# A new order for a mixer's products: keys and receptances of both head groups first, values and pool as filling, and an output projection that starts with the recurrence's rows

## The chip, the cores and the metric

The kernel runs on one core of a Trainium2 chip. The metric is the device time in microseconds of one execution, taken from several runs; the profile is one further execution with the hardware profiler on.

## The reference

One layer of a hybrid decoder trunk on 256 tokens of width 2048, all in float32:

```
h = rms_norm(x, attn_norm);  z = h @ w_in                    # 2048 -> 4384
d = causal_multiscale_pool(z[:, :1024])                      # 4 windows
pool_out = (d @ pool_w, per window) * pool_scale
r, k, v, w, a, g = token_shift(z[:, 1024:], mu_shift)        # 16 heads of 64
decay, a, g from low-rank products of w, a, g;  kk = normalised k * k_k
per token:  S = S * decay + (S @ -kk) (kk * a)^T + v k^T;    y = S @ r
y = group_norm(y) * gn_g + gn_b + sum(r * k * r_k) * v;      rwkv_out = y * g
x = x + concat(pool_out, rwkv_out) @ w_out
x = x + relu(rms_norm(x) @ w_ffn_up)^2 @ w_ffn_down          # width 8192
x = x + sigmoid(rms_norm(x) @ w_ple_gate) * (p @ w_ple_proj)
return rms_norm(x, final_norm)
```

## The kernel before

Each weight matrix is streamed once in panels of 512 KB (two row tiles of 128 by 512 columns). A panel is loaded into a ring `raw`, and split into a high part by ScalarE (`wh`, line 168) and a remainder by VectorE (`wl`, line 169), each ring three deep in the mixer. Every product is then made of three matmuls: high by high, high by low, low by high. `gemm_cols` keeps the output columns on the partitions (lines 181 to 183: zk, zr, zv), `gemm_toks` the tokens (lines 190 to 192: the pool's zp and w_out's o). Both take two of three PSUM banks `mm`; the next product can begin on the third, and goes on when the first two have been evacuated.

The mixer is about the first quarter of the run. In it the order of TensorE is written out by hand (`manual_schedule`): its matmuls run in the order in which the program issues them. The other engines, and the queue of DMA issues (SP), are ordered by a scheduler by priorities and its own estimates; evacuations and splits have raised priority.

The 16 heads are two groups (index 0 and 1) of eight. The recurrence is computed in four chunks of 64 tokens. The steps of a group, in the order of the program:

- `rwkv_lora`: low-rank products (L529), sigmoids, a running sum, two exponentials on ScalarE.
- `rwkv_k`: squares, sums over heads (`kkn`), a root, their spread (`rnb`, L497), and VectorE's products into the tiles AR and BK. It fills 6.4 and 4.6 us between these. `rwkv_r`: the same for r, and `rk`.
- `rwkv_scores`: chunk scores `sc` (L623), masked by VectorE into SC, with 2.6 us of filling between the chunks. `rwkv_sources`: BK scaled and transposed (`bkt`, L653).
- `bonus_sums` (tile `bs`, one buffer) and `rwkv_values`: the spread of the bonus (`bon`, L497), and the transposed, centred values (`vt`, L747), copied to UV.

Then, for both groups at once: `inverse`, a triangular inverse of 32 by 32 blocks, 31 dependent pairs of VectorE operations between transposes; `rwkv_merge` (products `gm` and `qm`, lines 708 and 717, with ScalarE copies into T1G and SC); and `rwkv_core`. In each of its four steps the core makes `dy`, evacuates R, makes `us` from R, evacuates UV (half on ScalarE, half on VectorE), updates the state from `us` and adds to `dy`. Behind these stand the fills whose sizes the change alters (1.5, 1.5, 1.8). After steps 1 and 3 `group_norm` treats one half of the tokens.

The tail of the mixer: `pool_chunk` (band products `pd`, lines 920 and 924), `group_out` (transposes `yt`, line 868, with scale and bias), `pool_mix` (`pm`), `rwkv_gates` (`gt`, lines 887 and 891) from the weight tile `gu`, which has one buffer and is loaded by `gate_load`, and `rwkv_out`, which multiplies the gates in and splits the result into `mg`. w_out takes its 16 row tiles from `mix`: 0 to 7 are the pool's (`mp`), 8 to 15 the recurrence's (`mg`); a panel covers two of them (`kps`).

The filling works by generators. Each `gemm_` function yields after a unit (0.36 us for column products, 0.68 for token products). `queued` puts it on a list; `fill(us)` takes units from the head of the list until the amount is reached or the list is empty; `finish(gen)` takes units until that product is done; `run` does a product at once. While the inverse is pending (`beside`), every 1.0 us of units also issues its next step, so `while beside: fill(1.0)` goes on until all its steps are issued. Before, the list is zk0, zr0, zv0, zk1, zr1, zv1, zp0, zp1; later two pieces of the first quarter of w_out (its pool rows) are queued as well and fill the tail.

Of the kernel before, what the change touches and what calls it, by code (L numbers as in the profile page):

```python
# [16 lines left out]
T = 256  # L17
# [23 lines left out]
def trunk(  # L41
# [221 lines left out]
    def fill(us):  # L263

        while us > 0 and queue:
            us -= advance()

    def finish(gen):
        while any(g is gen for g in queue):
            advance()  # L270
# [451 lines left out]

    def bonus_sums(gi, st):
        nb = head_sums(st["rk"], "bsum", 1)
        st["bs"] = rp.tile([128, T], F32, tag="sq", name=f"bs{gi}")
        with tc.high_priority(30000):
            nc.scalar.activation(st["bs"], nb, AF.Copy)

# [23 lines left out]
    def rwkv_core(sts):  # L752

        Rs = rp.tile([128, 2, 8, 64], F32, tag="tD", name="R")
        yss = [rp.tile([128, 2, 8, 64], F32, tag=tg, name=f"ys{gi}") for gi, tg in enumerate(("tE", "zv"))]
        SCs, UVs, ARs, BKts = ([st[k] for st in sts] for k in ("SC", "UV", "AR", "BKt"))

        def half(b, rows, part):
            return b[rows, part * 256 : part * 256 + 256]

        def direct(bs, c, p):
            for e in range(2):
                for gi in range(2):
                    h = 2 * p + e
                    nc.tensor.matmul(
                        half(bs[e], u_rows[gi], 0)[:, p * 64 : p * 64 + 64],
                        SCs[gi][v_rows[gi], a_slot[gi], c, h, :], UVs[gi][c][v_rows[gi], h, :],
                        start=p == 0, stop=c == 0, skip_group_check=True,
                    )

        def through_state(c, cur, bs, part):
            for p in range(4):
                for gi, e in ((0, 0), (1, 1), (1, 0), (0, 1)):
                    r = slice(e * 64, e * 64 + 64)
                    nc.tensor.matmul(
                        half(bs[e], (u_rows, v_rows)[part][gi], part)[:, p * 64 : p * 64 + 64],
                        ARs[gi][r, p, c, (a_slot, r_slot)[part][gi], :], cur[r, gi, p, :],
                        start=False, stop=False, skip_group_check=True,
                    )

        def by_parity(t_):
            return t_.rearrange("s (p e) i -> s e p i", e=2)

        def quarter(b):
            return b.rearrange("s (p i) -> s p i", i=64)

        bs = [rw_bank(f"dy{e}") for e in range(2)]
        for p in range(4):
            direct(bs, 0, p)
        norms = []  # L790
        for c in range(4):
            cur, nxt = states[c % 2], states[(c + 1) % 2]
            if c > 0:
                through_state(c, cur, bs, 0)
            R = Rs[:, c % 2]
            with tc.high_priority(30000):
                for e in range(2):
                    nc.scalar.activation(by_parity(R)[:, e], quarter(half(bs[e], slice(0, 128), 0)), AF.Copy)
                if 0 < c < 3:
                    nc.vector.tensor_tensor(nxt, cur, pcs[:, :, :, c : c + 1].to_broadcast([128, 2, 4, 64]), op=ALU.mult)  # L800
            if c > 0:
                through_state(c, cur, bs, 1)
            fill(1.5)
            us = rw_bank("us")
            bn = [rw_bank(f"dy{e}") for e in range(2)] if c < 3 else None
            for h in range(8):
                for gi in range(2):
                    nc.tensor.matmul(
                        us[u_rows[gi], h * 64 : h * 64 + 64], SCs[gi][u_rows[gi], a_slot[gi], c, h, :], R[u_rows[gi], h, :],
                        start=True, stop=True,  # L810
                    )
                if c < 3 and h % 2:
                    direct(bn, c + 1, h // 2)
            with tc.high_priority(30000):
                nc.scalar.activation(flat3(UVs[0][c])[LO], us[LO, :], AF.Copy)
                nc.vector.tensor_copy(flat3(UVs[1][c])[HI], us[HI, :])
            fill(1.5)
            if c < 3:
                for gi in range(2):
                    for h in range(8):  # L820
                        e, p = h % 2, h // 2
                        o = gi * 256 + p * 64
                        nc.tensor.matmul(
                            us[e * 64 : e * 64 + 64, o : o + 64], BKts[gi][c][:, p, e * 64 : e * 64 + 64], UVs[gi][c][:, h, :],
                            start=True, stop=True,
                        )
                add = us.rearrange("j (g p i) -> j g p i", g=2, i=64)
                with tc.high_priority(30000):
                    if c == 0:
                        nc.scalar.activation(nxt, add, AF.Copy)  # L830
                    else:
                        nc.vector.tensor_tensor(nxt, nxt, add, op=ALU.add)
            for h in range(8):
                p, e = h // 2, h % 2
                for gi in range(2):
                    nc.tensor.matmul(
                        half(bs[e], v_rows[gi], 1)[:, p * 64 : p * 64 + 64], SCs[gi][:, r_slot[gi], c, h, :], UVs[gi][c][:, h, :],
                        start=False, stop=True, skip_group_check=True,
                    )
            for gi in range(2):  # L840
                rows = slice(c % 2 * 64, c % 2 * 64 + 64)
                for e in range(2):
                    nc.scalar.activation(by_parity(yss[gi][rows, c // 2])[:, e], quarter(half(bs[e], v_rows[gi], 1)), AF.Copy)
            bs = bn
            if c < 3:
                fill(1.8)
            if c % 2:
                norms.append([group_norm(gi, c // 2, yss[gi][:, c // 2]) for gi in range(2)])
        return norms
# [25 lines left out]
    def gate_load(gi):  # L875
        raw = rp.tile([128, 768], F32, tag="gu", name=f"gu{gi}")
        nc.sync.dma_start(raw[:, 0:512], g_up[0:128, gi * 512 : (gi + 1) * 512])
        for half in range(2):
            c0 = gi * 512 + half * 256
            nc.sync.dma_start(raw[half * 32 : half * 32 + 32, 512:768], g_up[128:160, c0 : c0 + 256])  # L880
        return raw
# [79 lines left out]

    zk0, p_zk0 = z_product(4, "zk", "mu_k", 0)
    zr0, p_zr0 = z_product(2, "zr", "mu_r", 0)
    zv0, p_zv0 = z_product(6, "zv", "mu_v", 0)
    zk1, p_zk1 = z_product(4, "zk", "mu_k", 1)
    zr1, p_zr1 = z_product(2, "zr", "mu_r", 1)
    zv1, p_zv1 = z_product(6, "zv", "mu_v", 1)
    pool, mixes, xr = [], [], []
    p_zp0 = queued(gemm_toks(w_in[0], hT, "zp0", lambda banks: pool.append(pool_in(0, banks))))
# [23 lines left out]
    rwkv_scores(0, st0)  # L993
    rwkv_sources(0, st0)
    bonus_sums(0, st0)
    finish(p_zv0)
    fill(4.0)
    st1 = rwkv_lora(1)
    rwkv_values(0, st0, zv0[0])
    finish(p_zk1)  # L1000
    rwkv_k(1, st1, zk1[0])
    finish(p_zr1)
# [3 lines left out]
    sts = (st0, st1)  # L1006
    beside += [inverse(sts), 1.0, 0.0]
    rwkv_sources(1, st1)
    bonus_sums(1, st1)
    finish(p_zv1)  # L1010
    gu = gate_load(0)
    fill(4.0)
    rwkv_values(1, st1, zv1[0])
    while beside:
        fill(1.0)
    rwkv_merge(sts)
    fill(3.0)
    norms = rwkv_core(sts)
    finish(p_zp1)
    xr.extend(a8(3 + tt, f"x{tt}") for tt in range(2))  # L1020
    for tt in range(2):
        nc.sync.dma_start(xr[tt], x[tt * 128 : (tt + 1) * 128, :])
    YTs = [yb(gi, 1) for gi in range(2)]
    pws = [pool_weights(i) for i in range(2)]
    ds0 = pool_chunk(0, pool[0])
    for gi in range(2):
        group_out(gi, 0, norms[0][gi], YTs[gi])
    ds1 = pool_chunk(1, pool[1])
    mixes.append(pool_mix(0, ds0, pws[0]))
    o0 = [mm_bank(f"o0_b{i}") for i in range(2)]  # L1030
    p_o0 = [queued(gemm_toks(w_out[0], mix, "o0", None, kps, (), o0, kps[0] == 0, False)) for kps in ((0, 1), (2, 3))]
    fill(1.4)
    for gi in range(2):
        group_out(gi, 1, norms[1][gi], YTs[gi])
    mixes.append(pool_mix(1, ds1, pws[1]))
    mgs = []
    for gi in range(2):
        banks = rwkv_gates(gu)
# [2 lines left out]
        mgs.append(a8(gi, f"mg{gi}", F32R))  # L1041
        rwkv_out(YTs[gi], sts[gi]["rk"], banks, mgs[gi])
        fill(3.0)
    finish(p_o0[0])
    finish(p_o0[1])
    mixes += mgs
    order.close()
    rctx.close()
    fp = ctx.enter_context(tc.tile_pool(name="fp", bufs=1))
# [54 lines left out]

    h2_part, h2 = transposed("h2")
    for n in range(4):
        done = lambda banks: residual(banks, n)
        if n == 0:
            run(gemm_toks(w_out[n], mix, f"o{n}", done, (4, 5, 6, 7), (), o0, False))
        else:  # L1110
            run(gemm_toks(w_out[n], mix, f"o{n}", done))
        h2_part("mlp_norm", n)


# [335 lines left out]
```

## Time and profile before

| | |
|---|---|
| median of 3 runs | 1205.12 us |
| the runs | 1204.33, 1205.12, 1208.4 us |
| the profiled execution's own time | 1204.27 us |
| its span, first to last instruction | 1202.6 us |
| TensorE matmul busy | 1168.5 us, 97% |
| VectorE busy | 843.3 us, 70% |
| ScalarE busy | 669.6 us, 56% |
| mean granted TensorE clock | 0.993 |
| read from memory | 213.59 MB, 179 GB/s over the span |

The span lies 1.67 us below the execution's own time. PE is TensorE's matmul, PEld its weight load, DVE VectorE, ACT ScalarE, POOL GpSimd, SP the queue that issues the loads. A row of instructions gives start and duration in us, the engine, the line of the kernel, the operation, output and inputs by the program's names, shapes and a count, and in brackets the idle time ahead of it with what ended it. Matmuls are pipelined, so several in a row overlap in these durations. "PEclk" is the share of full clock that TensorE was granted.

### The profile page before, as it was taken

How to read it: one execution, taken by the hardware profiler on the slowest of the kernel's cores; microseconds unless marked ns; L12 is line 12 of the kernel's file. 1: busy time of each engine (PE TensorE's matmuls, PEld its weight loads, DVE VectorE, ACT ScalarE, POOL GpSimd, SP SyncE). 2: the span in 40 equal slices, each digit the busy share in tenths (PEclk: the TensorE clock that was granted, in tenths of full speed). 3: DMA queues.
4: the chain of work that ended last, by engine and by line, in shares of the span. 5: the costliest groups of instructions: out<-in, count | busy, mean ns of one | idle time of the engine just before them, and what ended most of it. 6: DMA issues, size and time to landing. Idle time of an engine off the chain costs nothing.

```text
span 1202.6 us, 18847 instructions
## 1 busy us (share of the span) xinstructions
PE 1168.5 (97%) x7314; PEld 999.3 (83%) x7314; DVE 843.3 (70%) x1105; ACT 669.6 (56%) x1204; POOL 19.7 (2%) x79
## 2 busy tenths in 40 slices
PE   7999999988999999999999999999999999999997
PEld 5998998767888888888887888888888888887886
DVE  6885578835655666666788788666667789788753
ACT  5956755566544555555545555455555555568743
POOL 4100000000000000000000000000000000000000
PEclk9999999989999999999999999999999999999999
DMA  7354453540655556656556657655655666665741
GB/s 276 123 188 138 144 172 121 202 135 19 189 189 184 185 177 192 187 183 191 187 190 203 208 176 221 198 184 185 192 181 178 202 197 206 229 203 202 262 146 70
DMA packets 60617, 216.91 MB, mean 180 GB/s; under 512 B 6768, under 2 KB 7536, under 8 KB 60144
## 3 DMA queue, kind: packets, MB, share of 16 engines
q1 hardware_dynamic: 60240, 215.20, 55.1%
q8 instruction: 57, 0.93, 0.3%
q10 hardware_dynamic: 288, 0.51, 0.1%
q14 instruction: 32, 0.26, 0.1%
HBM read 213.59 MB, written 2.10 MB: 179 GB/s over the span
## 4 chain that ended last, share of the span: by engine, by line
PE 79%; DVE 10%; DMA 5%; ACT 4%; issue 2%; DVEq 0%; ACTq 0%
PE u_w L1071 20%; PE u_w L1075 10%; PE d_p L1144 9%; DMA raw_d<-in_w_ffn_down_dram 5%; PE d_d L1144 2%; PE o_b L192 2%; PE o_b L190 2%; PE d_w L1144 2%; PE o_b L191 2%; PE gt_b L192 2%; PE gt_b L190 2%; PE gt_b L191 2%; PE wag_b L368 2%; DVE wl_d L169 1%; PE zp_b L190 1%
## 5 line engine op out<-in xcount | busy, mean ns | idle before, releaser
L1071 PE MATMUL u_w<-h,wh_u 128*128 128x512 f32 x1024 | 362.1, 399 | 0.0
L1075 PE MATMUL u_w<-h,wl_u 128*128 128x256 f32 x1024 | 287.7, 281 | 0.0
L168 ACT ACTIVATE wh_u<-raw_u 128x512 fp32r<-128x512 f32 x256 | 147.6, 624 | 174.6 <-issue 135.4
L169 DVE TENSOR_TENSOR wl_u<-raw_u,wh_u 128x1024 fp32r<-128x1024 f32 x128 | 156.6, 1224 | 122.0 <-ACT wh_u L168 121.9
L1071 PEld LDWEIGHTS u_w<-h,wh_u 128*128 128x128 f32 x1024 | 192.5, 188 | 47.9
L1075 PEld LDWEIGHTS u_w<-h,wl_u 128*128 128x128 f32 x1024 | 193.4, 189 | 0.0
L1144 PE MATMUL d_p<-wh_d,yd 128*128 128x512 f32 x480 | 154.6, 390 | 1.1 <-ACT wh_d L168 0.8
L168 ACT ACTIVATE wh_d<-raw_d 128x512 fp32r<-128x512 f32 x160 | 89.2, 620 | 36.5 <-issue 16.7
L1144 PEld LDWEIGHTS d_p<-wh_d,yd 128*128 128x128 f32 x480 | 90.1, 188 | 20.6 <-ACT wh_d L168 1.8
L169 DVE TENSOR_TENSOR wl_d<-raw_d,wh_d 128x1024 fp32r<-128x1024 f32 x80 | 95.4, 1220 | 14.1 <-ACT wh_d L168 13.7
L1144 PE MATMUL d_p<-wl_d,yd 128*128 128x512 f32 x240 | 93.6, 390 | 0.1
L169 DVE TENSOR_TENSOR wl_o<-raw_o,wh_o 128x1024 fp32r<-128x1024 f32 x32 | 39.1, 1225 | 40.2 <-ACT wh_o L168 40.2
L1144 PE MATMUL d_d<-wh_d,yd 128*128 128x512 f32 x160 | 55.7, 389 | 0.0
L168 ACT ACTIVATE wh_o<-raw_o 128x512 fp32r<-128x512 f32 x64 | 36.7, 623 | 32.4 <-PE o_b L192 17.8
L1144 PEld LDWEIGHTS d_p<-wl_d,yd 128*128 128x128 f32 x240 | 45.0, 188 | 10.2 <-DVE wl_d L169 1.1
L1197 ACT ACTIVATE th_d<-t_d 128x1024 fp32r<-128x1024 f32 x24 | 25.4, 1060 | 46.2 <-DVE t_d L1194 40.0
L1144 PE MATMUL d_w<-th_d,ys 128*128 128x512 f32 x144 | 48.2, 389 | 0.0
L1201 ACT ACTIVATE th_d<-t_d 128x1024 fp32r<-128x1024 f32 x24 | 25.4, 1059 | 34.9 <-DVE t_d L1199 23.6
L1202 DVE TENSOR_TENSOR tl_d<-t_d,th_d 128x1024 fp32r<-128x1024 f32 x24 | 29.4, 1224 | 19.9 <-ACT th_d L1201 19.6
L1191 ACT ACTIVATE w7h_d<-raw_d 128x1024 fp32r<-128x1024 f32 x24 | 25.4, 1059 | 27.1 <-DMA raw_d<-in_w_ffn_down_dram 11.7
L192 PE MATMUL gt_b<-wh_gt,h 128*128 128x512 f32 x96 | 37.8, 393 | 0.0
L190 PE MATMUL gt_b<-wh_gt,h 128*128 128x512 f32 x96 | 37.5, 390 | 0.0
(524 smaller groups left out, 2538.5 us busy)
## 6 DMA issues: line engine op xcount, KB each, us to landing
raw_u<-in_w_ffn_up_dram SPq DMA_DIRECT2D x128, 512.0 KB, 3.5
raw_d<-in_w_ffn_down_dram SPq DMA_DIRECT2D x128, 512.0 KB, 4.0
raw_o<-in_w_out_dram SPq DMA_DIRECT2D x32, 512.0 KB, 3.6
raw_gt<-in_w_ple_gate_dram SPq DMA_DIRECT2D x24, 512.0 KB, 4.3
raw_zk<-in_w_in_dram SPq DMA_DIRECT2D x16, 512.0 KB, 3.5
raw_zr<-in_w_in_dram SPq DMA_DIRECT2D x16, 512.0 KB, 3.6
raw_zv<-in_w_in_dram SPq DMA_DIRECT2D x16, 512.0 KB, 4.3
raw_zp<-in_w_in_dram SPq DMA_DIRECT2D x16, 512.0 KB, 3.5
```

What stands on the lines that cost most here:

```text
L168: nc.scalar.activation(wh[:, a * 512 : (a + 1) * 512], raw[:, a * 512 : (a + 1) * 512], AF.Copy)
L169: nc.vector.tensor_tensor(wl, raw, wh.bitcast(F32), op=ALU.subtract)
L190: nc.tensor.matmul(o, a_h, wh[:, 0:n], start=first, stop=False)
L191: nc.tensor.matmul(o, a_h, wl[:, 0:n], start=False, stop=False)
L192: nc.tensor.matmul(o, a_l, wh[:, 0:n], start=False, stop=last)
L1071: nc.tensor.matmul(bank[:, ct, :].rearrange("p (s t) -> p s t", s=2), wh[:, c], hl, start=k == 0, stop=False, skip_group_check=True,)
L1075: nc.tensor.matmul(bank[:, ct, 0:T], wl[:, c], hl[:, 0, :], start=False, stop=k == 15, skip_group_check=True)
L1144: nc.tensor.matmul(o, l, r, start=first, stop=last, skip_group_check=True)
L1191: nc.scalar.activation(ha, ra, AF.Copy)
L1197: nc.scalar.activation(th[0], t[0], AF.Copy)
L1201: nc.scalar.activation(th[1], t[1], AF.Copy)
L1202: nc.vector.tensor_tensor(tl[1], t[1], th[1].bitcast(F32), op=ALU.subtract)
```

## The change

The list becomes zk0, zr0, zk1, zr1, zv0, zv1, zp0, zp1. Group 1's low-rank step, k and r follow directly on group 0's. Both groups' values come behind the start of the inverse, and the first gate load behind group 1's values; since the bonus sums of group 0 now live across group 1's k, `bs` moves to the buffer `gu`. The core's fills are 2.4 us each. Behind the core only pool chunk 0 is made ahead of the normalised output; then come both halves of `group_out`, the gates and `rwkv_out` of both groups, the mix of pool 0, and the whole first quarter of w_out in the order of row panels 4, 5, (pool chunk 1), 6, 7, (mix of pool 1), 0, 1, 2, 3, with the residual added at its end. The load of x moves behind the gates in the program. No product is added or dropped.

```diff
 def bonus_sums(gi, st):
-        st["bs"] = rp.tile([128, T], F32, tag="sq", name=f"bs{gi}")
+        st["bs"] = rp.tile([128, T], F32, tag="gu", name=f"bs{gi}")
...
 def rwkv_core(sts):                      # in each of the four steps
             if c > 0:
                 through_state(c, cur, bs, 1)
-            fill(1.5)
+            fill(2.4)
             us = rw_bank("us")
...
-            fill(1.5)
+            fill(2.4)
             if c < 3:
...
             if c < 3:
-                fill(1.8)
+                fill(2.4)
...
     zr0, p_zr0 = z_product(2, "zr", "mu_r", 0)
-    zv0, p_zv0 = z_product(6, "zv", "mu_v", 0)
     zk1, p_zk1 = z_product(4, "zk", "mu_k", 1)
     zr1, p_zr1 = z_product(2, "zr", "mu_r", 1)
+    zv0, p_zv0 = z_product(6, "zv", "mu_v", 0)
     zv1, p_zv1 = z_product(6, "zv", "mu_v", 1)
...
     bonus_sums(0, st0)
-    finish(p_zv0)
-    fill(4.0)
     st1 = rwkv_lora(1)
-    rwkv_values(0, st0, zv0[0])
     finish(p_zk1)
...
     beside += [inverse(sts), 1.0, 0.0]
     rwkv_sources(1, st1)
+    finish(p_zv0)
+    fill(4.0)
+    rwkv_values(0, st0, zv0[0])
     bonus_sums(1, st1)
     finish(p_zv1)
-    gu = gate_load(0)
     fill(4.0)
     rwkv_values(1, st1, zv1[0])
+    gu = gate_load(0)
     while beside:
         fill(1.0)
     rwkv_merge(sts)
     fill(3.0)
     norms = rwkv_core(sts)
-    finish(p_zp1)
-    xr.extend(a8(3 + tt, f"x{tt}") for tt in range(2))
-    for tt in range(2):
-        nc.sync.dma_start(xr[tt], x[tt * 128 : (tt + 1) * 128, :])
     YTs = [yb(gi, 1) for gi in range(2)]
-    pws = [pool_weights(i) for i in range(2)]
+    pws = [pool_weights(0)]
     ds0 = pool_chunk(0, pool[0])
     for gi in range(2):
         group_out(gi, 0, norms[0][gi], YTs[gi])
-    ds1 = pool_chunk(1, pool[1])
-    mixes.append(pool_mix(0, ds0, pws[0]))
-    o0 = [mm_bank(f"o0_b{i}") for i in range(2)]
-    p_o0 = [queued(gemm_toks(w_out[0], mix, "o0", None, kps, (), o0, kps[0] == 0, False)) for kps in ((0, 1), (2, 3))]
-    fill(1.4)
+    fill(4.0)
     for gi in range(2):
         group_out(gi, 1, norms[1][gi], YTs[gi])
-    mixes.append(pool_mix(1, ds1, pws[1]))
     mgs = []
     for gi in range(2):
         banks = rwkv_gates(gu)
...
         rwkv_out(YTs[gi], sts[gi]["rk"], banks, mgs[gi])
         fill(3.0)
-    finish(p_o0[0])
-    finish(p_o0[1])
-    mixes += mgs
+    finish(p_zp1)
+    xr.extend(a8(3 + tt, f"x{tt}") for tt in range(2))
+    for tt in range(2):
+        nc.sync.dma_start(xr[tt], x[tt * 128 : (tt + 1) * 128, :])
+    mixes += [pool_mix(0, ds0, pws[0]), None] + mgs
+    o0 = [mm_bank(f"o0_b{i}") for i in range(2)]
+
+    def out0(*kps):
+        return gemm_toks(w_out[0], mix, "o0", lambda banks: residual(banks, 0), kps, (), o0, 4 in kps, 2 in kps)
+
+    run(out0(4, 5))
+    pws.append(pool_weights(1))
+    ds1 = pool_chunk(1, pool[1])
+    run(out0(6, 7))
+    mixes[1] = pool_mix(1, ds1, pws[1])
+    run(out0(0, 1))
+    run(out0(2, 3))
     order.close()
...
     for n in range(4):
-        done = lambda banks: residual(banks, n)
-        if n == 0:
-            run(gemm_toks(w_out[n], mix, f"o{n}", done, (4, 5, 6, 7), (), o0, False))
-        else:
-            run(gemm_toks(w_out[n], mix, f"o{n}", done))
+        if n:
+            run(gemm_toks(w_out[n], mix, f"o{n}", lambda banks: residual(banks, n)))
         h2_part("mlp_norm", n)
```

## The prediction

> **What bounds the kernel now.** I read the page first, then the waits of the matmul engine, then its busy time and granted clock by stretch, then the time lines of the engines around the mixer.
>
> ```profile
> span 1202.6 us, 18847 instructions
> PE 1168.5 (97%) x7314; PEld 999.3 (83%) x7314; DVE 843.3 (70%) x1105; ACT 669.6 (56%) x1204; POOL 19.7 (2%) x79
> ```
>
> TensorE is busy for 1168.5 of 1202.6 us, so the kernel is a row of matmuls, and a change of order (no product is added or dropped) can win only what that row loses: 34.1 us in all. The waits of TensorE say where (columns: total us, times, longest).
>
> ```profile
> PE us L823 <- DVE UV L816: 4.0, 2, 2.6
> PE qm L717 <- ACT T1G L710: 3.7, 2, 3.4
> PE dy L775 <- ACT R L798: 3.2, 3, 1.3
> PE zp_b L190 <- DVE zv_t L332: 1.8, 1, 1.8
> PE dy L836 <- ACT UV L815: 0.8, 1, 0.8
> PE dy L836 <- DVE UV L816: 0.7, 1, 0.7
> PE dy L775 <- ACT state L830: 0.2, 1, 0.2
> ```
>
> These are the mixer's (the rest lies at the start and the end of the kernel, which the change does not reach): after the inverse (qm) 3.7, in the recurrence's core 8.9 (4.0 + 3.2 + 0.8 + 0.7 + 0.2), at the start of the pool products 1.8. There is one more loss, which no wait shows, the clock. In the rows of stretches the columns are the busy us of PE, PEld, DVE, ACT, POOL, then the granted clock, the DMA share and GB/s.
>
> ```profile
> 186.30:233.10 46.80, 45.05 (x246) 37.32 (x244) 42.82 (x88) 26.36 (x46) 0.00 (x0) 1.00 0.46 153
> 238.20:241.60 3.40, 0.05 (x1) 0.00 (x0) 0.62 (x1) 3.33 (x6) 0.00 (x0) 0.95 0.89 359
> 241.60:251.90 10.30, 9.98 (x143) 8.32 (x143) 3.13 (x4) 6.40 (x11) 0.00 (x0) 0.52 0.35 105
> 251.90:282.50 30.60, 21.71 (x689) 18.65 (x688) 12.27 (x18) 15.26 (x38) 0.00 (x0) 1.00 0.29 94
> 282.50:322.90 40.40, 40.19 (x225) 33.40 (x225) 26.49 (x39) 25.22 (x56) 0.00 (x0) 1.00 0.37 120
> ```
>
> From 241.6 to 251.9 us TensorE was granted 0.52 of its clock: 10.3 us, of which 10.3 x 0.48 = 4.9 us are lost at most. It follows a stretch of 3.4 us with next to no matmul. The stretch 251.9 to 282.5 is the core: only 21.7 of 30.6 us busy. In the last stretch, 282.5 to 322.9 us (pool, normalisation, gates, first quarter of w_out), TensorE has 40.2 of 40.4 us busy: there is almost nothing to win there, but its order is changed too.
>
> **Filling, before and after.** A product of a queue is cut into units (0.36 us each in column products, 0.68 in token products by the code's own numbers), and a fill takes whole units. The inverse is emitted over 40 us of filling. Before: 5.04 + 2.16 of the values, then pool units, until 40.1 of the pool's 43.5 us (2 x 32 units) are gone when the core begins; its first two fills take the last 3.4 us, and the other nine are empty. After: the inverse gets 5.04 + 2.16 of group 0's values, 4.32 + 18.72 of group 1's, and only 4.08 + 6.80 of the pool; the merge takes 6.12; so 26.5 us are left to the core, which asks 2.72 (four units) eleven times: the ninth is the last full one, the first fill of step 3 gets 2.04. The second fill of step 3, the 4.0 behind the first normalised half and both 3.0 behind the gates are empty. In before that stretch was filled from w_out's pool rows, which now come behind it.
>
> **The core.** The fills stand behind the us products and behind the update of the state; the wait for R stands ahead of its fill. So the 4.0 us for UV in steps 1 and 2 go (2.72 us against a longest wait of 2.6), and the 0.2 for the state. Step 3's 0.8 + 0.7 stay. The three waits for R (3.2) stay in kind; ScalarE copies ys ahead of R today and would do that during the fill, so I take 2.2 and bound it by 1.5 and 4.5 (weight splits of the pool now run on ScalarE beside it). Each entry into a fill costs:
>
> ```profile
> 253.14 0.50 PE L190 MATMUL zp_b<-wh_zp,hTh 128*128 128x512 f32 x1
> ...
> 253.48 0.40 PE L191 MATMUL zp_b<-wl_zp,hTh 128*128 128x512 f32 x1
> ...
> 255.43 0.27 PE L808 MATMUL us<-R,SC 64*64 64x64 f32 x2
> ```
>
> The first pool matmul lasts 0.50 instead of 0.40, and three units (2.04) take 253.14 to 255.43 = 2.29 us: 0.25 for each fill. Eight more fills, 2.0 us, less the switches saved elsewhere; I take 1.6. Core: -4.0 - 0.2 - 1.0 + 1.6 = -3.6 us (-5.5 to -1).
>
> **Values of group 0.** They leave the place right behind the second low-rank step (lora).
>
> ```profile
> 116.82 2.49 PE L497 MATMUL bon<-bs,hsel 32*128 32x256 f32 x8
> ...
> 200.46 0.71 PE L497 MATMUL bon<-bs,hsel 32*128 32x256 f32 x8
> ...
> 201.11 2.11 PE L747 MATMUL vt<-cen,zv_t 128*128 128x128 f32 x16
> ...
> 195.28 0.48 DVE L332 SCALAR_TENSOR_TENSOR zv_t<-zv_b,par_sb,zv_t 128x255 f32<-128x255 f32 x1
> ...
> 201.59 1.41 DVE L733 TENSOR_TENSOR tF_t<-bon,zv_t 128x256 f32<-128x256 f32 x4
> ```
>
> In the first place the bonus spread took 2.49 us, for group 1 0.71: it waited for banks that the low-rank step still held (TensorE shows it as busy). Behind the inverse's start that cause is gone: -1.8 us. The move adds work beside the inverse: on TensorE 0.65 + 1.9 us, on VectorE four evacuations of 0.48 and 1.41 of bonus, 3.3 us, where VectorE is already 42.8 of 46.8 us busy up to the merge (the chain is its own). So qm comes 3.3 later, TensorE only 2.7: the wait for qm grows by 0.6. The change of banks from values to values costs a part of the 1.8 us that values to pool cost; a column product works longer on its first bank, so +0.4 (0 to 1.8).
>
> **Group 1's preparation.** Between the low-rank step and the end of the k product there were 18 us of filling, now 1.4; group 0 has 5.0. Group 0's rows (ScalarE, without a gap there):
>
> ```profile
> 49.66 0.86 ACT L533 ACTIVATE tD_t<-la,par_sb 128x256 f32<-128x256 f32 x2
> ...
> 50.54 1.28 ACT L538 ACT_TABLE_LOAD   x1
> ...
> 51.85 1.06 ACT L538 ACTIVATE tA_t<-tB_t 128x1024 f32<-128x1024 f32 x1
> ...
> 52.82 1.14 ACT L168 ACTIVATE wh_zr<-raw_zr 128x512 fp32r<-128x512 f32 x2
> ...
> 54.81 0.81 ACT L331 ACTIVATE zk_t<-zk_b,omu 128x256 f32<-128x256 f32 x2
> ...
> 56.75 1.71 ACT L550 ACTIVATE tF_t<-zk_t,par_sb 128x256 f32<-128x256 f32 x4
> ```
>
> From the low-rank step to the spread of the norms TensorE has about 17 us. ScalarE must do in it 8 sigmoids (0.43 each), two table loads and a third for the root (1.28 each), two exponentials (1.06), 4 evacuations and 4 squares (0.42 each) = 12.8 us, and six weight splits of 1.14: 19.6 us. That is 2.6 us too much, less the panels split ahead of the step. I take +1.0 (0 to 4). The bonus sums now share the gate's buffer, which costs nothing by itself; but the moved gate load waits on the DMA queue for the bonus spread of group 1, with pool loads behind it; the splits run two or three panels of 2.7 us ahead, so nothing (0 to 2).
>
> **The tail, where the change pays.** Rows of the core's last product, pool, transposes, normalisation (DVE), gates, and the reload of the gate weights:
>
> ```profile
> 281.37 1.15 PE L836 MATMUL dy<-UV,SC 128*64 128x64 f32 x30 [0.72 <-DVE UV L816]
> ...
> 282.44 0.51 PE L920 MATMUL pd<-wband,zt 128*128 128x144 f32 x2
> ...
> 284.42 1.04 PE L868 MATMUL yt<-ident,ys 128*128 128x128 f32 x8
> ...
> 287.22 0.69 DVE L862 TENSOR_TENSOR ys<-ys,gv 128x512 f32<-128x512 f32 x1
> ...
> 288.06 0.69 DVE L862 TENSOR_TENSOR ys<-ys,gv 128x512 f32<-128x512 f32 x1
> ...
> 297.16 1.89 PE L887 MATMUL gt<-zf,gu 128*128 128x256 f32 x8
> ...
> 298.98 1.13 PE L891 MATMUL gt<-zf,gu 32*128 32x256 f32 x8
> ...
> 300.18 0.33 SPq L877 DMA_DIRECT2D gu<-in_g_up_dram  x1
> ...
> gu<-in_g_up_dram SPq DMA_DIRECT2D x1, 256.0 KB, 2.7
> ...
> PEld o_b L192 <- DVE mp L955: 1.0, 2, 0.6
> ```
>
> From the last dy (end 282.5) TensorE has pool chunk 0 and the first transposes, to 285.4: 2.9 us. The second half's norms end 287.9 and 288.75 (VectorE, L862), 5.4 and 6.3 us after the core. Now nothing lies between: 2.5 + 0.4 = 2.9 us of wait (before: pool chunk 1, the mix of chunk 0 and three units of w_out). Then the second transposes, 1 us, and the gates of group 0, 3.0 us. Their weights have one buffer: the reload is issued at 300.18, when the last gate product (298.98 + 1.13) is done, and takes 2.7 us. Before, a fill of five units (3.4 us) covered that. Now TensorE stands for the 2.7 and the step to the queue, 2.8 us. Behind the second gates the mix of pool chunk 0 covers the output of group 1, and w_out's rows 4, 5 find theirs ready. The later pool half lies between w_out's row pairs, 5.4 us each: covered. Gone are waits of w_out for the fresh pool mix (1.0). Tail: 2.9 + 2.8 - 1.0 = +4.7 us (2 to 7). What is late next is w_out's weights: w_out's later panels, and x, are written behind the gate reload on the DMA queue, which stands there until the gates are done; the first panels find idle DMA time in the core (share 0.29), and x is needed only by the residual, 20 us and more later. So nothing, 3 us if that cover is gone.
>
> **The sum** against the profiled execution's own 1204.27 us (span 1202.6 and 1.67 around it): core -3.6, values -1.8, qm +0.6, bank change +0.4, group 1 +1.0, tail +4.7 = +1.3, so 1205.6. The median of the runs, 1205.12, lies 0.85 above that execution; in such runs 1206.4 us.
>
> **The clock.** One loss is not in the sum, since I leave it as it is.
>
> ```profile
> 241.62 0.31 PE L717 MATMUL qm<-SC,T1G 32*32 32x32 f32 x2 [3.37 <-ACT T1G L710]
> ...
> 242.23 3.62 PE L717 MATMUL qm<-SC,T1G 32*32 32x32 f32 x126 [0.30 <-ACT T1G L710]
> ```
>
> The half clock begins with the end of a wait of 3.37 us; waits of 2.6 in the core did not bring it. The wait at qm stays (4.3 by my sum), so the 4.9 us stay. The Trainium skill (TensorE: Matmul & The Clock Gate, Part 1) says that the gate halves the clock after an idle window of about 3.4 us, free-running, and opens it after a busy one. The trace agrees with the 3.4; its slow stretch was three times as long as one window. By the page a second event, if one came in the tail, would cost 1.7 us (an estimate: half of one window), and the slower rival below would be 1208.7; by the rows it is 1211.2. The tail's two waits of the sum are each under 3 us, below the one wait that brought the half clock; what is doubtful is that they lie some 4 us apart and that the first is cut only by transposes.
>
> **Rivals.** *Slower: the tail loses the clock too.* It decides when the norms or the gate reload come 0.6 us later than in the rows, which makes one wait 3.4. Price: the longer wait, and another stretch of 4.9 at most (I take 4.2): 1206.4 + 0.6 + 4.2 = 1211.2 us. For it: ScalarE and VectorE also do w_out's splits there. Against: the core has two waits within 10 us at clock 1.00. Chance 0.25. *Slower: ScalarE after the second low-rank step.* At the full 4 us instead of 1, 1209.4, more with scores late; chance 0.13. *Faster: the inverse ends earlier against TensorE.* If the wait at qm falls to 2 us, because T1G's copies come sooner, the half clock goes with it: -2.3 - 4.2 = 1199.9 us. For it: on ScalarE a weight split stands ahead of the copies of T1G that qm waits for, and in another order its 1.14 us are gone; TensorE comes later by 2.7. Against: VectorE, on which the inverse runs, gets 3.3 us more. Chance 0.20, together with a tail at its lower bound. *The change doesn't do what it says* (the filling never reaches the core) would leave 8.9 us in the core and add the tail: 1210; the unit count speaks against it, and it is in the slower cases.
>
> **How the numbers follow.** 0.3% (3.6 us) is about what a measurement of this kernel can tell from no change; the three runs span 4.1. Within it (1201.5 to 1208.7) lies the forecast of a trade, 0.42, likeliest 1206.4, its own range 1202 to 1209. Slower 0.25 + 0.13 = 0.38; faster 0.20. For 8 in 10 the range takes in the clock in the tail with its spread and the inverse without its stretch: 1199.5 to 1213.5.
>
> **What would show it.** Right: no wait of us for UV in steps 1 and 2, pool products through step 3; waits of yt and of gt for gu in the tail, 2 to 4 us each; bon at 0.7 twice; qm still waiting and the clock half behind it. Wrong: gates and transposes without a wait; a clock of 0.5 behind the core; waits of rnb or the k and r products on ScalarE at about 110 to 130 us.

## The result and the profile after

| | before | after |
|---|---|---|
| median of 6 runs | 1205.07 us | 1209.95 us |
| the runs | 1204.03 to 1208.4 us | 1208.27 to 1212.0 us |
| the profiled execution's own time | 1204.27 us | 1208.27 us |
| its span | 1202.6 us | 1206.6 us |
| mean granted TensorE clock | 0.993 | 0.992 |

The changed kernel is slower: 1.0039 times the time of the one before, 95% interval [1.0022, 1.0056], or 4.7 us (2.7 to 6.7). The forecast of a trade, 1206.4, was 3.5 us too low. The profiled execution is the quickest of the six and has the highest mean clock (0.992; the others 0.989 to 0.990), so the trace below shows rather less lost to the clock than the median run lost.

The waits of TensorE up to the end of the mixer, after, without that for the first weights at the start (total us, times, longest):

```profile
PE qm L717 <- ACT T1G L710: 3.0, 4, 1.7
PE gt L887 <- DMA gu<-in_g_up_dram: 2.9, 1, 2.9
PE zp_b L190 <- DVE zv_t L332: 2.1, 1, 2.1
PE yt L868 <- ACT ybuf L870: 2.1, 1, 2.1
PE dy L775 <- ACT R L798: 2.0, 3, 1.1
PE zr_b L181 <- DVE zk_t L332: 1.7, 2, 1.3
PE dy L836 <- DVE UV L816: 1.2, 1, 1.2
PE dy L836 <- ACT UV L815: 1.1, 1, 1.1
PE zr_b L183 <- DVE wl_zr L169: 0.3, 1, 0.3
PE zv_b L181 <- DVE zv_t L332: 0.3, 1, 0.3
PE yt L868 <- DVE ys L862: 0.2, 1, 0.2
```

The wait of `us` for UV, 4.0 us before, has no row any more. New are the rows of the tail (`gt`, and `yt` twice) and, in group 1's preparation, 1.3 of the 1.7 us of `zr_b` and the 0.3 below it; the other 0.4 is group 0's and was there before. The time line of TensorE in the tail, with the idle time ahead of a row and its releaser in brackets:

```profile
279.59 1.45 PE L836 MATMUL dy<-UV,SC 128*64 128x64 f32 x30 [1.18 <-DVE UV L816]
280.97 0.85 PE L920 MATMUL pd<-wband,zt 128*128 128x144 f32 x2
...
284.23 1.04 PE L868 MATMUL yt<-ident,ys 128*128 128x128 f32 x8
287.33 0.63 PE L868 MATMUL yt<-ident,ys 128*128 128x128 f32 x4 [2.06 <-ACT ybuf L870]
...
288.63 1.89 PE L887 MATMUL gt<-zf,gu 128*128 128x256 f32 x8
290.45 1.13 PE L891 MATMUL gt<-zf,gu 32*128 32x256 f32 x8
294.47 3.37 PE L887 MATMUL gt<-zf,gu 128*128 128x256 f32 x8 [2.89 <-DMA gu<-in_g_up_dram]
...
329.04 0.33 PE L1097 MATMUL h2t<-ident,x 128*128 128x128 f32 x1
```

Two things are to be seen. The waits are where the prediction put them (2.06 and 2.89 us). And the same eight gate products take 1.89 us for group 0 and 3.37 for group 1; the first pool product takes 0.85 where it took 0.51 before. That is the clock: both run in stretches that were granted half of it. The next view has the grid on which it changes (columns as in the prediction: busy us of the engines, granted clock, DMA share, GB/s):

```profile
215.39:218.81 3.42, 1.75 (x9) 1.13 (x7) 1.23 (x1) 3.33 (x6) 0.00 (x0) 1.00 0.51 158
218.81:222.22 3.41, 2.08 (x92) 1.75 (x94) 1.23 (x1) 3.31 (x6) 0.00 (x0) 1.00 0.36 132
222.22:229.05 6.83, 6.83 (x61) 5.55 (x55) 0.00 (x0) 2.04 (x5) 0.00 (x0) 0.50 0.21 77
276.83:280.25 3.42, 1.12 (x30) 0.85 (x26) 1.92 (x2) 1.20 (x3) 0.00 (x0) 1.00 0.84 331
280.25:283.66 3.41, 3.41 (x28) 3.29 (x24) 0.69 (x1) 2.50 (x6) 0.00 (x0) 0.50 0.65 267
283.66:287.07 3.41, 1.61 (x14) 1.37 (x13) 2.67 (x5) 2.76 (x9) 0.00 (x0) 1.00 0.00 0
290.49:293.90 3.41, 1.09 (x9) 0.64 (x8) 3.25 (x6) 2.00 (x5) 0.00 (x0) 1.00 0.26 88
293.90:297.31 3.41, 2.84 (x7) 2.33 (x8) 0.97 (x2) 0.24 (x1) 0.00 (x0) 0.50 0.05 13
```

Behind 276.83 and 290.49, windows in which TensorE worked 1.1 of 3.4 us, the next whole window is at half clock. The second holds the wait for `gu`, 2.89 us. The first lies ahead of the tail: it holds the two waits of the core's step 3 for UV, 1.12 and 1.18 us. The window with the wait of `yt` (from 283.66, 1.61 us of work) was followed by full clock. Read stretch by stretch, the tail (first `pd` to first `h2t`) took 282.44 to 323.46 = 41.02 us before and 280.97 to 329.04 = 48.07 after: +7.05.

### The profile page after: what moved, and what is told of

It is laid out like the page before. It is cut to its first block, busy times and chain, and to the rows that moved or that the text cites. A ratio compares the mean times of both kernels' runs of the same rounds, so it can differ in the third digit from the quotient of the medians.

```text
span 1206.6 us, 18842 instructions
## 1 busy us (share of the span) xinstructions
PE 1171.0 (97%) x7314; PEld 1001.0 (83%) x7314; DVE 843.1 (70%) x1105; ACT 670.5 (56%) x1204; POOL 19.7 (2%) x79
## 4 chain that ended last, share of the span: by engine, by line
PE 87%; DVE 5%; ACT 4%; DMA 3%; issue 1%; DVEq 0%; ACTq 0%
PE u_w L1076 20%; PE d_p L1146 14%; PE u_w L1080 10%; PE d_w L1146 4%; PE d_d L1146 4%; PE o_b L192 2%; PE o_b L190 2%; PE o_b L191 2%; DMA raw_d<-in_w_ffn_down_dram 2%; PE gt_b L192 2%; PE gt_b L191 2%; PE gt_b L190 2%; PE wag_b L368 2%; PE zp_b L190 1%; PE zp_b L192 1%
## 5 line engine op out<-in xcount | busy, mean ns | idle before, releaser
L169 DVE TENSOR_TENSOR wl_zp<-raw_zp,wh_zp 128x1024 fp32r<-128x1024 f32 x16 | 19.5, 1217 | 29.7 <-ACT wh_zp L168 29.7
L181 PE MATMUL zr_b<-hTh,wh_zr 128*128 128x256 f32 x128 | 36.8, 288 | 1.7 <-DVE zk_t L332 1.7
```

The source lines that it names most:

```text
L169: nc.vector.tensor_tensor(wl, raw, wh.bitcast(F32), op=ALU.subtract)
L181: nc.tensor.matmul(o, w_h, ah, start=first and ct % 2 == 0, stop=False, skip_group_check=True)
```

## The experiments

Theory A: the new order of front and core wins as meant, and the tail eats it, by its two waits and by the half clock they bring. Rival B: the loss lies in front and core, and the tail is nearly free. Each ratio is against the kernel before, run on the same chip in the same turn.

**The two halves apart.** The first kernel has the new list, core fills and front, and the old code from the core's end on; the second is the kernel before with the new tail alone (from `pws = [pool_weights(0)]` to the last `run(out0(2, 3))`, and the first w_out quarter out of the later loop).

```diff
     norms = rwkv_core(sts)
+    finish(p_zp1)                              # first kernel: as before the change
...
-    fill(4.0)
+    ds1 = pool_chunk(1, pool[1])
+    mixes.append(pool_mix(0, ds0, pws[0]))
...
+    p_o0 = [queued(gemm_toks(w_out[0], mix, ...)) for kps in ((0, 1), (2, 3))]
+    fill(1.4)
...
```

> The changed kernel's front and core, with the tail of before (pool half and w_out's pool rows as filling between the normalised halves and the gates). Theory A (the tail's two waits and the half clock that comes with them eat what front and core win): the 7.0 us that the tail grew go, less the 1.5 us that later stages gave back: about 1204, the transposes and gates without a wait, clock 1.00 behind the core. Rival B (the loss sits in the front and the core: group 1's preparation and the entries into more fills; the tail is neutral): stays at 1209 to 1210.

> The kernel before, with only the tail of the changed kernel (both normalised halves, the gates, then pool mix and the whole first quarter of w_out). Theory A: 1205.1 + 5 to 7 = 1210 to 1212, with waits of about 2 us for the normalised half and 2.9 for the gate reload. Rival B: 1205, within 1 us of before.

Measured: the new front with the old tail 1202.6 us, ratio 0.9976 [0.9964, 0.9989]; the new tail alone 1213.44, ratio 1.0065 [1.0041, 1.0089]. So the front and core win 2.9 us and the tail loses 7.8; their sum, +4.9, is the whole change within its interval. B falls. One expectation of A failed, though: with the old tail, whose transposes and gates have no wait, the clock behind the core is still half for one window:

```profile
275.33:278.75 3.42, 1.12 (x28) 0.84 (x26) 1.92 (x2) 1.59 (x4) 0.00 (x0) 1.00 0.84 286
278.75:282.16 3.41, 3.41 (x38) 3.29 (x33) 0.34 (x1) 2.00 (x5) 0.00 (x0) 0.50 0.79 318
```

So this window belongs to the core's step 3 and not to the tail. In the new tail alone, from the waits of TensorE:

```profile
PE gt L887 <- DMA gu<-in_g_up_dram: 2.8, 1, 2.8
...
PE yt L868 <- DVE gv L861: 2.6, 1, 2.6
```

**The gate weights' one buffer.** The changed kernel, with group 1's gate weights in a buffer of their own (that of BKt, free when the core ends), loaded ahead of the gates:

```diff
-        raw = rp.tile([128, 768], F32, tag="gu", name=f"gu{gi}")
+        raw = rp.tile([128, 768], F32, tag=("gu", "BKt")[gi], name=f"gu{gi}")
...
+    gus = [gu, gate_load(1)]
...
-        banks = rwkv_gates(gu)
-        if gi == 0:
-            gu = gate_load(1)
+        banks = rwkv_gates(gus[gi])
```

> The changed kernel; group 1's gate weights get a buffer of their own (that of BKt, free behind the core), and are loaded at the core's end. Theory A: the wait of 2.9 us for the reload and the half clock behind it (1.5) go: 1205.5 to 1207. Rival B: the wait only moves to the next thing that is late (the pool mix's or the output's operands): 1209 to 1210.

Measured: 1205.28 us, ratio 1.0000 [0.9985, 1.0014], 4.7 us better than the whole change. The wait for `gu` is gone from its waits. That is more than the 2.9 of the wait, but the intervals of the two ratios (1.0014 and 1.0022 at their near ends) leave anything from about 1 us on, so the surplus is not shown by the times. Nor does the profile show the half clock gone, as A had it: it stands in three windows in and just ahead of the tail (277.62 to 284.45 and 287.86 to 291.27 us), the last behind the wait of `yt`, which is still there (1.9 us). This profile is of one of the slower executions, 1207.32 us.

**Filling left for the tail.** The changed kernel, with the fill ahead of `us` in the core's first step alone; so 7.5 us of pool units are left behind the core:

```diff
-            fill(2.4)
+            if c == 0:
+                fill(2.4)
             us = rw_bank("us")
```

> The changed kernel without the fills behind the wait for R in steps 1 to 3 (they stand behind the wait and hide nothing): 7.5 us of pool units are left over and go to step 3's second fill, the 4.0 behind the first normalised half and the 3.0 behind the first gates. Theory A: step 3's 2.3 us, most of the 2.3 for the normalised half, and part of the 2.9 for the gates go, with the clock: 1202 to 1205. Rival B (what binds is the chain through ScalarE and VectorE, and filling only moves the waits): 1208 to 1210.

Measured: 1203.47 us, ratio 0.9983 [0.9971, 0.9995]. The waits of `yt` and of step 3 for UV are gone, R is waited for as before (2.0 us: what was taken away had covered nothing). What is left in the tail is the gate reload, with three windows of half clock around and behind it (285.39 to 295.63 us):

```profile
PE gt L888 <- DMA gu<-in_g_up_dram: 3.0, 1, 3.0
```

**Both.** The two edits together.

> The changed kernel with both cures of its tail: the fills behind the waits for R left out in steps 1 to 3 (pool units reach the tail), and a second buffer for the gate weights. Theory A: against the run with the first cure alone (1203.5) the wait of 3.0 us and the 10 us at half clock behind it go: 1196 to 1199. Rival B (the gate's wait is followed by another of the same length, for the output's operands): 1202 to 1203.5.

Measured: 1197.29 us, ratio 0.9940 [0.9927, 0.9953]. The tail has neither wait, and no half clock; its gates run at 1.89 us both times:

```profile
279.84 1.89 PE L888 MATMUL gt<-zf,gu 128*128 128x256 f32 x8
...
283.53 1.89 PE L888 MATMUL gt<-zf,gu 128*128 128x256 f32 x8
```

So the new order can beat the one before. What the two edits took away together is 0.99% of the time (1.0039 to 0.9940): the two waits of the tail, step 3's two for UV, and what the clock added. Whether the new tail is better than the old one with the same fills in the core, no run shows; the fastest version below has the old tail.

**Group 1's preparation.** The changed kernel, with group 1's low-rank step one place earlier, between the scores and the sources of group 0:

```diff
     rwkv_scores(0, st0)
+    st1 = rwkv_lora(1)
     rwkv_sources(0, st0)
     bonus_sums(0, st0)
-    st1 = rwkv_lora(1)
```

> The changed kernel with group 1's low-rank step one fill earlier, ahead of group 0's sources, so that 5.0 us more of filling stand between it and the end of group 1's k product. If ScalarE's load after that step makes the waits of 1.3 and 0.3 us in group 1's r product, as theory A has it, they go: 1210 - 1.6 = 1208.3. If ScalarE is late for another reason (the splits' own pace), they stay: 1210.

Measured: 1208.85 us, ratio 1.0038 [1.0024, 1.0051]: no difference to the whole change that can be told. The cause was met: group 1's waits in `zr_b` (1.3 and 0.3 us) are gone, `rnb` now waits 0.7. The core begins at 226.40 us instead of 229.63, but 1.75 of these 3.2 us lie ahead of the first `zk` product (25.84 instead of 27.59 us), which the edit does not touch. From the core's beginning to the first `h2t` it takes 102.4 instead of 99.4 us: in this profile the half clock in the tail lasted three windows (290.50 to 300.74) instead of one.

**The wait at qm.** The kernel before, with a longer fill in the merge:

```diff
-        fill(2.6)
+        fill(6.0)
```

> The kernel before; the last 3.4 us of pool units stand in the merge, ahead of qm, instead of in the core's step 0. Theory A (a wait that leaves a clock window of 3.4 us less than half busy costs its length and then half of 3.4 to 10 us more): the wait of 3.4 and the half clock of 10 us go, 2.1 us of waits for R and UV come to step 0: 1205.2 - 3.4 - 4.2 + 2.1 = 1199.7. Rival B (the clock falls anyway, at the next low window): 1205.2 - 3.4 + 2.1 = 1203.9.

Measured: 1205.26 us, ratio 1.0008 [0.9997, 1.002]. The wait is gone and nothing was won; both theories missed. Its waits and grid windows:

```profile
PE us L823 <- DVE UV L816: 5.9, 3, 2.6
...
PE us L808 <- ACT R L798: 0.8, 1, 0.8
...
PE qm L717 <- ACT T1G L710: 0.4, 1, 0.4
```

```profile
241.51:244.92 3.41, 3.02 (x131) 2.42 (x130) 1.52 (x2) 3.29 (x7) 0.00 (x0) 1.00 0.38 117
244.92:248.34 3.42, 3.42 (x9) 2.68 (x10) 1.71 (x3) 2.66 (x5) 0.00 (x0) 0.50 0.60 172
...
268.82:272.23 3.41, 0.95 (x64) 0.81 (x54) 2.94 (x6) 1.25 (x3) 0.00 (x0) 1.00 0.02 5
272.23:275.64 3.41, 3.24 (x60) 3.25 (x62) 0.80 (x2) 0.00 (x0) 0.00 (x0) 0.50 0.00 0
```

The units spent in the merge are missing in the core, where the waits grow by 1.9 + 0.8 us; and the half clock, one stretch of 10.24 us before, is now four of 3.41 (from 244.92, 255.16, 272.23 and 282.47 us). So a wait of 3.4 us was not its only cause. New theory: the clock is set per window of 3.41 us, by how busy TensorE was in it. If so, matmuls that nobody needs must help.

**Extra matmuls.** `junk(n)` issues n matmuls (128x512) into a bank that nobody reads; they fill waits, and the data waited for come no sooner. First in the kernel before, then in the tail of the changed one.

```diff
+    def junk(n):
+        b = mm_bank("junk")
+        for _ in range(n):
+            nc.tensor.matmul(b, hT_h[0][:, 0:128], hT_h[0][:, 0:512], start=True, stop=True)
...
+        junk(14)                               # before: ahead of qm
...
+            if c:
+                junk((0, 5, 11, 5)[c])         # before: behind UV in the core's steps 1 to 3
...
+    junk(9)                                    # changed: behind fill(4.0), ahead of the second half
...
+        if gi == 0:
+            junk(12)                           # changed: behind the first gates
```

> The kernel before with 35 extra matmuls (128x512, into a bank that nobody reads): fourteen ahead of qm, and 5, 11 and 5 behind UV in the core's steps 1, 2 and 3. No wait of the data is shortened. Theory (the clock is set by how busy TensorE was in windows of 3.41 us): the half clock that follows qm's wait of 3.4 us, 10.24 us long, goes, which is worth up to 4.9: about 1200.5 of 1205.1. Rival (it is set by something else, or it only moves to another stretch, as with the longer merge fill): 1205.

Measured: 1200.51 us, ratio 0.9961 [0.995, 0.9973]. Thirty-five matmuls more make the kernel 4.7 us faster (3.3 to 6.0). The place of the old half clock, before and with the extra products:

```profile
237.84:241.26 3.42, 0.41 (x2) 0.00 (x0) 0.28 (x1) 3.37 (x5) 0.00 (x0) 1.00 0.98 399
241.26:251.50 10.24, 9.58 (x142) 8.13 (x143) 3.47 (x4) 6.71 (x12) 0.00 (x0) 0.50 0.35 108
```

```profile
237.00:240.40 3.40, 3.27 (x15) 2.38 (x13) 0.59 (x1) 3.34 (x5) 0.00 (x0) 1.00 0.89 369
240.40:250.60 10.20, 9.76 (x196) 7.86 (x199) 3.43 (x5) 8.23 (x15) 0.00 (x0) 1.00 0.46 132
```

The stretch of 10.2 us behind the wait at qm, at 0.50 before, is at 1.00. That the data come no sooner can be read too: ScalarE's last copy of T1G ends 10.3 us behind the start of the first `gm` product in both kernels. From that product to the core's first `dy` it takes 15.1 us instead of 19.0 (231.94 to 247.05, 233.09 to 252.06), and the core takes 30.5 instead of 30.4. The clock follows the busy share, and the theory's number was met.

> The changed kernel with 21 extra matmuls (128x512, into a bank that nobody reads): nine behind the last pool units before the first yt transposes, twelve behind the first gates' products. They shorten no wait; they only keep TensorE busy in it. Theory (the clock is set by how busy TensorE was in windows of 3.41 us): the two half-clock windows of the tail go, which cost 1.3 (pd) and 1.4 (the second gates), so -2.7 of 1210.0: about 1207.3, if the extra products end before what they wait beside. Rival (the clock has nothing to do with the busy share, the slow products there have another reason): 1210 or, where the extra products reach past the waits, up to 2 more.

Measured: 1208.02 us, ratio 1.0030 [1.0019, 1.0041]; the interval overlaps that of the change itself, so the times alone do not show a gain. The trace does, at one of the two places:

```profile
275.30:278.71 3.41, 1.11 (x28) 0.83 (x26) 1.92 (x2) 1.70 (x4) 0.00 (x0) 1.00 0.83 292
278.71:282.13 3.42, 3.42 (x38) 3.30 (x37) 0.14 (x1) 1.81 (x5) 0.00 (x0) 0.50 0.81 326
...
288.95:292.37 3.42, 3.42 (x19) 2.39 (x18) 3.40 (x6) 2.00 (x6) 0.00 (x0) 1.00 0.21 54
292.37:295.78 3.41, 3.41 (x17) 2.39 (x18) 1.30 (x3) 0.74 (x2) 0.00 (x0) 1.00 0.12 41
```

Behind the gates' wait the clock stays at 1.00, and the second gates take 1.97 us where they took 3.37. The other half-clock window stays, and my expectation had its cause wrong: the idle window ahead of it is that of the core's step 3 (the two waits for UV), before the first of the extra products. Only one of the 1.3 and 1.4 us could go, and the tail is 46.3 us (280.36 to 326.66) instead of 48.07.

**A version that beats both.** The changed front and core with the old tail, the fill ahead of `us` in the first step alone, group 1's low-rank step early, and the merge's fill at 6.6 instead of 2.6: each edit as above, no extra matmuls.

> The changed kernel's front and core with the tail of before, the low-rank step of group 1 one fill earlier, no fills behind the waits for R, and 4 us of the pool units so saved in the merge ahead of qm (6.6 instead of 2.6). Theory A: against the run with the old tail (1202.6): group 1's waits -1.6, the wait for qm -2 to -3 and its half clock -2 to -3, step 3's waits -2.3: 1193 to 1196. Rival B (the chains through ScalarE and VectorE bind, and filling only moves the waits): 1200 to 1202.

Measured: 1191.06 us, ratio 0.9892 [0.9875, 0.9910]. Of the waits in the mixer, R (2.2), `zp_b` (2.1) and one of 1.5 at the pool chunk are the largest, and half clock is left for two windows of 3.41 us.

## Why the prediction was right, and where it was wrong

The time, 1209.95, lies in the range 1199.5 to 1213.5, but not in the part that was called a trade (up to 1208.7) and given the best chance. By the prediction's own bounds the slower outcome came, given 0.38, and the range holds because it took in the clock in the tail. Of its signs of being wrong two were seen: a clock of 0.5 behind the core, and the r product waiting at 113 to 121 us. In the profiled executions the time rose by 4.0 us (1204.27 to 1208.27); the sum had +1.3. Step by step, from the two time lines:

| step of the prediction | forecast | measured |
|---|---|---|
| core | -3.6 | -2.1 |
| values of group 0 | -1.8 | -1.7 |
| wait at qm | +0.6 | -1.3 |
| bank change | +0.4 | +0.8 |
| group 1's preparation | +1.0 | +2.0 |
| tail | +4.7 | +7.05 |
| not in the sum: start of the kernel | 0 | +0.8 |
| not in the sum: after the mixer | 0 | -1.5 |

**The tail.** The two waits were right in place and nearly in size (2.06 + 0.21 against 2.9; 2.89 against 2.8); the first was ended by ScalarE's copy of the first transposes, 0.15 us behind the norm that the prediction had named, and its 0.21 by the norm of the other group. Taken without waits and clock, the rest of the tail became about 0.8 us shorter, where the sum had 1.0 for w_out's waits. The step that failed is the one on the clock: "The tail's two waits of the sum are each under 3 us, below the one wait that brought the half clock". What counts is not the length of one wait but the busy share of a fixed window, and windows with 1.12 and 1.09 us of work were enough. One of the two lies where the prediction did not look: step 3's waits for UV, in the core, brought the half clock on the pool products, also with the old tail. The other holds the wait for `gu`. The price: 1.3 us on the pool products (first `pd` to first `yt` 3.26 instead of 1.98) and 1.4 on the second gates (294.47 to 298.83 = 4.36, where the first took 3.0). These 2.7 us are as much as the whole error of the sum (4.0 against 1.3), but that is chance: the other rows of the table are off by up to 1.9 us, and cancel.

The rival "the tail loses the clock too" named this mechanism for the tail, with a condition (a wait of 3.4) that was not needed. Its time, 1211.2, is nearer than the sum's. The doubt that the two waits lie some 4 us apart did not decide: the window of the first was followed by full clock. The rule of the Trainium skill (TensorE: Matmul & The Clock Gate, Part 1), a free-running window of about 3.4 us, agrees with the grid of 3.413 us in the trace; that the window has to be idle does not, with 1.12 and 1.09 us of work in these two.

**The core.** The 4.0 us for UV and the 0.2 for the state went, and R fell to 2.0 (2.2 in the sum). Two sizes were off. Step 3's 0.8 + 0.7, which I let stay, became 1.12 + 1.18. VectorE's rows show what stands ahead of its copy to UV, the split of a w_out panel:

```profile
277.58 1.23 DVE L169 TENSOR_TENSOR wl_o<-raw_o,wh_o 128x1024 fp32r<-128x1024 f32 x1 [1.97 <-ACT wh_o L168]
278.84 0.69 DVE L816 COPY UV<-us 64x512 f32<-64x512 f32 x1
```

TensorE was idle from 276.96 us, so the copy starts 1.9 us behind its last product; before, behind a split of pool weights, it was 1.1 (279.52 to 280.62). The prediction let w_out's first panels land in the core and counted nothing for their splits there. And with -4.0 - 0.2 - 1.2 + 0.8 = -4.6 for the waits, 2.5 are left for the entries into the fills and, in the last `dy`, for the clock (1.45 us for its 30 products instead of 1.15); I had 1.6, after taking 0.4 off for switches saved; that the switches cost more is what remains by subtraction, and no run isolates it.

**The wait at qm.** It fell where I let it grow: the largest is 1.7 instead of 3.4 us. The rival "the inverse ends earlier against TensorE" so came true in its first half. Its second half, "If the wait at qm falls to 2 us ... the half clock goes with it", did not: behind two windows with 1.75 and 2.08 us of work the clock is half from 222.22 to 229.05, and the fifteen pool products that follow take 6.25 us, as before (6.28).

**Group 1's preparation.** ScalarE was late, as said: it works without a gap from 106.55 to 122 us, and `zr_b` waits 1.31 us for the evacuations of zk_t and 0.33 for a split. Moving the step one place earlier took these away. The term was right in kind, half of what was measured, far from the 4 us of the rival. One sum beside it does not come out: 0.65 + 1.9 us on TensorE are 2.55, not the 2.7 that the wait at qm was reckoned from; it moves that term by 0.15.

**Values and banks.** `bon` takes 0.71 us in its new place (173.79 us), as forecast. The bank changes wait 0.32 and 2.13 us where 1.75 was.

The 0.8 us at the start lies ahead of everything that the change touches (the first `zk` product stands at 27.59 instead of 26.82 us). Most of it is the clock: the first full clock comes at 14.01 us instead of 12.56, and the 48 products of `wag_b` that run then take 14.78 instead of 14.13 us. In the kernel before with extra matmuls, whose code is the same there, it came at 10.44 and they took 13.15. What was given back after the mixer is partly two waits of the FFN-down products, 0.8 us for their weights and 0.3 for x, that are absent after, while one for x in `pp_b` grew from 0.3 to 0.7; the rest I did not follow, and no run isolates it.

## What to carry to other kernels

A queue of filling is a budget: count where each unit goes and where the list runs empty, for filling moved into one wait leaves another one open, and here the waits left open at the end of the list, in the core's last step and in the tail, cost more than the filled ones brought. Look at busy time in the clock's own windows and not at the longest wait, since a short wait amid sparse work can halve the clock for the dense products behind it. Give a weight tile that is reloaded between two uses a second buffer before its cover is taken away.

## What the runs showed of the hardware

In all profiles the granted clock changes on a grid of 3.413 us, whose phase against the kernel's start is not the same in all runs, and in the mixer half clock lasts one, two or three windows (3.41, 6.83, 10.24 us). Over the mixers of the twelve kernels every window at full clock with 1.3 us or less of matmul work, 14 of them, was followed by half clock; of those between 1.4 and 2.1 some were and some were not (1.41 before: not; 1.44 above, in the merge kernel: yes), and what decides there stays open. The longest idle stretch in a window does not decide either: 1.18 us in the changed kernel's window from 276.83, which was followed by half clock, and 2.00 in the window with 1.41 us of work, which was not. Above 2.1 it came once, behind a window with 3.02 us of busy time that were mostly the 32 by 32 products of `qm`: it looks as if small products count for less, but no run isolates that.

The phase probably also makes runs of one kernel differ. The kernel with two gate buffers ran twelve times: seven at a mean clock of 0.994, median 1204.04 us, and five at 0.989 to 0.991, median 1207.32. That the grid's phase makes this difference of 3 us is not shown, since only one of the twelve was profiled, and at 0.994 alone the times span 6 us (1200.63 to 1206.75), so it is not the only cause of spread.
